# Shorter GpSimd subtractions, a short convolution kept in PSUM and an rsqrt with one instruction fewer, in a two-block transformer kernel

## The chip, the cores and the metric

The kernel runs on one core of one Trainium2 chip. The metric is the device time of one execution in microseconds; lower is better. Six parts of the core matter here: TensorE (PE; its weight loads are listed as PEld), VectorE (DVE), ScalarE (ACT), GpSimd (POOL), SyncE (SP), which issues most of the DMAs, and the two on-chip memories, SBUF and PSUM. GpSimd is used on SBUF tiles alone.

## The reference, cut to what matters

Input x has 512 tokens of 1024 features. Two layers of a first block and one layer of a second block follow one another, all in float32. Of the first block's mixer, the lines around the change are these:

```python
x_m, z, glu_a, glu_b = jnp.split(h @ w_in, ...)
x_c = jax.nn.silu(causal_depthwise_conv(x_m, w_conv_m, b_conv_m))   # 4 taps
q, k = einsum(x_c, w_q), einsum(x_c, w_k)
v = einsum(x_m, w_v)
h_m = sigmoid(z) * group_layer_norm(mlstm(q, k, v, gates))
a = glu_a * sigmoid(glu_b)
a = silu(group_layer_norm(causal_depthwise_conv(a, w_dw, b_dw)))    # 31 taps
y = concat([h_m, a]) @ w_out
```

A feed-forward stage (1024 to 4096 to 1024, squared ReLU) closes each layer. The second block has index attention over selected keys, window attention and a feed-forward stage. RMS and layer norms stand between the stages; each needs 1/sqrt of a mean.

## The kernel before, in words

**Products of split operands.** Each product is computed as three matmuls (mm3, lines 195 to 204). Both operands are split into a rounded part and a remainder. The rounded part is a ScalarE copy; the remainder is a subtraction on VectorE or GpSimd. For weights this is done in prep (173 to 180): a unit of 128 x 1024 arrives by DMA, ScalarE rounds it (177) and line 179 subtracts, on GpSimd for the units that the tables TUNE name under pool and on VectorE for the rest. AHEAD = 4 units are prepared ahead of use. For activations it is split (206 to 213); with pool set, line 210 runs on GpSimd. split_pair (695) sets it for the mixer's head inputs, 128 x 512 each, scores and split_hm set it where the table says so, and start sets it for every second feature tile.

**Stages.** mixer computes, feature-major, 8 tiles of x_m with their short convolution (ev_xm, 881), then heads, gates and the gated long convolution. The long convolution's taps (conv_gen, line 830) accumulate on VectorE into a PSUM bank of the ring py and are background work; conv_out norms each tile of it: transposes, rsqrt, ScalarE's scale (858), transposes back (862). values norms each head with rsqrt and ScalarE (802). In ev_xm, line 886 copies the product to xm on ScalarE, line 889 writes tap 0 with its bias into an SBUF tile, VectorE adds three taps, ScalarE takes Tanh (892). In the first layer, where mv[1] is 1, ScalarE adds 1 (894) and GpSimd multiplies (895); in the second layer one VectorE instruction does both.

**rsqrt** (215 to 236) is a chain of tiny VectorE instructions on up to four columns: halve, two integer instructions for a first guess, then two refining steps.

**What sets the order.** Paced (54) counts a rough time for each VectorE instruction, mm3 counts TensorE's. pump (132) issues background work (long-convolution taps, modulation sums at line 287, selection) while VectorE's count is no later than TensorE's plus slack. A scheduler then orders the instructions of each engine by priority (later, soon). Each engine works through its queue in order. Most weights are fetched from SyncE's queue, some modulation rows (298) from GpSimd's. PSUM has a ring p of five banks, py of two and pc of one; a product takes its bank when its first matmul is issued and gives it back after the last reader.

The lines shown as L68 in the profile are all VectorE instructions issued through Paced.

Of the kernel before, what the change touches and what calls it, by code (L numbers as in the profile page):

```python
# [21 lines left out]
MID = 3  # L22
CALM = True
# [17 lines left out]
NEG = -1e30  # L41
# [3 lines left out]
# the guess is 1.5 ** 0.2 / sqrt, for the cubic step to have a leading coefficient of 1  # L45
# [8 lines left out]
class Paced:  # L54
    """an engine whose instructions are counted, by their rough time"""
# [16 lines left out]
class Kern:  # L72
# [59 lines left out]
    def pump(self):  # L132
        """issue what fits in before VectorE would be later than TensorE"""
        again = True
        while again:
            again = False
            for b in (self.bg[-1:] + self.bg[:-1] if self.tune["af"] else self.bg):
                cost, at, cond = b[1]
                if self.pt < at or (cond and not cond()) or (cost and self.dt + cost > self.pt + self.tune["slack"]):
                    continue  # L140
                self.dt = max(self.dt, self.pt - 3) + cost
                self.step(b)
                again = True
                break

    def drain(self, done):
        """issue background work until done()"""
        while not done():
            for b in self.bg:
                cost, at, cond = b[1]  # L150
                if cond is None or cond():
                    self.dt += cost
                    self.step(b)
                    break
            else:
                raise RuntimeError("nothing left to drain")

# [1 line left out]
    def add_chunk(self, src, widths, pool=""):  # L159
        """pool: which of the remainders GpSimd computes"""  # L160
        o = 0
        for i, w in enumerate(widths):
            self.plan.append((src[:, o:o + w], w, str(i) in pool))
            o += w
# [8 lines left out]
    def prep(self, i):  # L173
        raw, w = self.units[i], self.plan[i][1]
        u = self.units[i] = self.tile("w", (128, 2, 1024), F32R)
        with self.later("prep"):
            self.nc.scalar.activation(u[:, 0, :w], raw[:, :w], AF.Copy)  # L177
            eng = self.nc.gpsimd if self.plan[i][2] else self.V
            eng.tensor_tensor(u[:, 1, :w], raw[:, :w], f32(u[:, 0, :w]), op=OP.subtract)  # L179
        self.prepped += 1  # L180
# [25 lines left out]
    def split(self, hi, lo, src, scale=None, pool=False):  # L206
        nc = self.nc
        if scale is None:
            nc.scalar.activation(hi, src, AF.Copy)  # L209
            (nc.gpsimd if pool else self.V).tensor_tensor(lo, src, f32(hi), op=OP.subtract)  # L210
        else:
            nc.scalar.activation(hi, src, AF.Copy if isinstance(scale, float) else AF.Identity, scale=scale)
            self.V.scalar_tensor_tensor(lo, src, scale, f32(hi), op0=OP.mult, op1=OP.subtract)

    def rsqrt(self, src, w, mul, add, tag=None):
        """1 / sqrt(src * mul + add), src [128, w]: a guess from the bits, a cubic and a quadratic step"""
# [12 lines left out]
        V.tensor_scalar(z.bitcast(I32), vh.bitcast(I32), 1, None, op0=OP.logical_shift_right)  # L229
        V.tensor_scalar(z.bitcast(I32), z.bitcast(I32), -1, RSQRT_GUESS, op0=OP.mult, op1=OP.add)  # L230
# [53 lines left out]
    def ada_sum(self, w, l, i):  # L284
        """mod[:, i] = w . silu(c), w the i-th 128 rows of w_ada^T"""
# [32 lines left out]
    def scale_cols(self, l, which):  # L318
        """g_pre * (1 + sc), and sh"""
# [7 lines left out]
    def gate_row(self, l, which):  # L327
        """gt * g_post, as a row on every partition"""
# [17 lines left out]
    def start(self, evacs):  # L346
        """the first normed operand by feature tile, as its scale and shift arrive, and the first products with it"""
# [91 lines left out]
    def norm_T(self, ii, xs, ss, G, sh, to):  # L439
        """rows of the token tiles from ii on, normed; transposed, scaled and split into hT two by two, as pend is worked off"""  # L440
# [48 lines left out]
    def feat(self, evacs, halves=False, hook=None, tag="p"):  # L489
        """128 outputs each: [128, T] = w^T h^T, handed to its evac"""  # L490
# [58 lines left out]
    def post_norm(self, l, which, nxt):  # L549
        """x += gt * rms_norm(y) * g_post; then the next normed operand"""  # L550
# [40 lines left out]
    def gate_weights(self, l):  # L591
        """Wq Wgq + Wk Wgk and Wv Wgv by head, as [feature, 8 gates]; in 4 steps"""
# [46 lines left out]
    def gates(self, l):  # L639
        """gate pre-activations by token -> log forget sums, and what the weights need; in 4 steps"""  # L640
# [89 lines left out]
    def weights_exp(self, h):  # L730
        """exp(a_s - M_t) for s <= t, by key tile"""
# [41 lines left out]
    def values(self, S, vt, h):  # L773
        """weighted sums of values, normed by head: [128 tokens, 4 tiles, 256]"""
# [42 lines left out]
    def conv_gen(self, l, inp, out):  # L817
        """the taps of the depthwise convolution, by channel tile"""
# [15 lines left out]
    def conv_out(self, l, c, yp, outs):  # L834
        """silu(norm over the 128 channels of the group)"""
# [35 lines left out]
    def mixer(self, l, nxt, halves=True):  # L871
# [9 lines left out]
        def ev_xm(j):  # L881
            def ev(p):
# [4 lines left out]
                y, th = self.t2(), self.t2()  # L887
# [5 lines left out]
                if self.tune["mv"][1]:  # L893
                    nc.scalar.activation(th, th, AF.Copy, bias=1.0)
                    nc.gpsimd.tensor_tensor(xc, th, y, op=OP.mult)
                else:
                    V.scalar_tensor_tensor(xc, th, 1.0, y, op0=OP.add, op1=OP.mult)
# [162 lines left out]
    def tok_proj(self, n, kks, evac):  # L1060
        """[128 tokens, n] = h w for each token tile"""
# [27 lines left out]
    def rotate(self, src, i, n, pool=False):  # L1089
        """rotary embedding of n heads of token tile i; src and result [128, n, 64]"""  # L1090
# [14 lines left out]
    def q_hold(self, i, p, hold, tag):  # L1105
        """query heads of a token tile, rotated: [tokens, head, rounded part and remainder]"""
# [6 lines left out]
    def q_turn(self, i, hold, qt, hps):  # L1113
        """token tiles i and i + 1 of two pairs of heads into qt"""
# [18 lines left out]
    def q_proj(self, tag):  # L1133
        """8 query heads: 4 tiles [rounded part; remainder of a head, 2 heads, T], once the turns are worked off"""
# [5 lines left out]
    def k_proj(self):  # L1140
        """index key, 2 + 2 key heads: [part twice; T] for the rounded part and the remainder"""
# [61 lines left out]
    def qk_mm(self, out, q, h, tk, k, keys):  # L1203
        """q . k from [q_h; q_l] and [k_h; k_h], [k_l; k_l]"""
# [24 lines left out]
    def select(self):  # L1229
        """in place of the scores: 0 for each query's 128 largest (the earliest among equals), NEG elsewhere"""  # L1230
# [12 lines left out]
    def scores_a(self, h, qt, kt):  # L1243
        """one head's probabilities over the selected keys, by query tile"""
# [51 lines left out]
    def scores_b(self, hp, qt, kt):  # L1296
        """two heads' probabilities in the window, by query tile"""
# [46 lines left out]
    def gate(self, t, tag):  # L1344
        """the next 128 gates, as tanh of their half"""
        self.feat([lambda p: self.nc.scalar.activation(t, p, AF.Tanh, scale=0.5)], tag=tag)

    def branch(self, j, w, o, tag="p"):
        """128 outputs of a branch: [128, T] = w^T o"""
# [178 lines left out]
# order of the 128-wide column tiles of w_in: 0-7 x_m, 8-15 z, 16-23 glu_a, 24-31 glu_b  # L1528
# [125 lines left out]
```

## Time and profile before

| what | value |
|---|---|
| median of 3 runs (range) | 2425.57 us (2423.27 to 2426.83) |
| profiled execution, first to last instruction | 2424.3 us, 1.3 us below the median |
| TensorE busy | 2252.7 us, 93% |
| VectorE busy | 1610.0 us, 66% |
| ScalarE busy | 976.7 us, 40% |
| GpSimd busy | 625.4 us, 26% |
| chain that ended last | PE 62%, DVE 24%, ACT 4%, POOL 1% |

The profiled execution lists no time of its own beside its span. Busy times are unions of the instructions' records on an engine. Matmuls are pipelined, so a busy TensorE isn't one at its peak. A wait is put down to the instruction whose semaphore came last.

### The profile page before, as it was taken

The numbers are of one execution on the slowest core, as the hardware profiler recorded it, in microseconds if no ns is written. First come the engines' busy times: TensorE is split into PE (matmuls) and PEld (weight loads), VectorE is DVE, ScalarE is ACT, GpSimd is POOL, SyncE is SP. The second block draws the span as 40 slices with busy tenths as digits, with TensorE's granted clock in tenths as the row PEclk, the third lists the DMA queues.
The fourth block names the chain that finished last, engine by engine and source line by source line (L and its number), as shares of the span: only waits on it lengthen the run. The fifth ranks groups of instructions, "written<-read, shape, count | busy, mean of one in ns | idle before, by whom it ended". The sixth has DMA issues, their size and how long they took to land.

```text
span 2424.3 us, 28416 instructions
## 1 busy us (share of the span) xinstructions
PE 2252.7 (93%) x10552; PEld 1828.9 (75%) x10552; DVE 1610.0 (66%) x2971; ACT 976.7 (40%) x1705; POOL 625.4 (26%) x408
## 2 busy tenths in 40 slices
PE   5988998899999998898897999999989999999998
PEld 4667776688888776776676888887877888888886
DVE  6899999755777669999956233347887435443444
ACT  3434554443232343455445333234436543422332
POOL 2733452313234243444322011012031231000000
PEclk9999999999999999999998999999999999999999
DMA  7523223526666422222133332223111223322222
GB/s 271 174 75 106 71 81 118 181 97 214 214 206 205 144 97 81 66 66 66 63 108 104 122 104 96 96 87 109 62 70 44 63 103 138 110 95 94 95 96 87
DMA packets 77754, 271.34 MB, mean 112 GB/s; under 512 B 9008, under 2 KB 9776, under 8 KB 77616
## 3 DMA queue, kind: packets, MB, share of 16 engines
q1 hardware_dynamic: 69840, 241.21, 29.9%
q0 software_dynamic: 7776, 28.32, 3.6%
q8 instruction: 83, 1.36, 0.2%
q14 instruction: 55, 0.45, 0.1%
HBM read 256.91 MB, written 12.58 MB: 111 GB/s over the span
## 4 chain that ended last, share of the span: by engine, by line
PE 62%; DVE 24%; ACT 4%; issue 2%; POOL 1%; DMA 1%; ACTq 0%; DVEq 0%; SPq 0%; POOLq 0%
PE p L197 19%; PE p L199 19%; PE p L198 19%; DVE p L830 7%; DVE c L68 5%; DVE cc L68 2%; DVE t L68 2%; DVE s L68 1%; DVE E L68 1%; PE p L466 1%; DVE w L68 1%; DVE e L68 1%; DVE ad L287 1%; DVE d L68 1%; DVE hT L68 0%
## 5 line engine op out<-in xcount | busy, mean ns | idle before, releaser
L179 POOL TENSOR_TENSOR w<-wr,w 128x1024 fp32r<-128x1024 f32 (+1 forms) x166 | 399.7, 2411 | 842.8 <-ACT w L177 739.3
L177 ACT ACTIVATE w<-wr 128x1024 fp32r<-128x1024 f32 (+1 forms) x353 | 368.9, 1047 | 572.1 <-PE p L199 517.2
L197 PE MATMUL p<-hT,w 128*128 128x512 f32 (+1 forms) x1504 | 582.7, 389 | 14.0 <-ACT hT L209 7.6
L198 PE MATMUL p<-hT,w 128*128 128x512 f32 (+1 forms) x1504 | 576.0, 383 | 8.0 <-DVE hT L68 5.6
L199 PE MATMUL p<-hT,w 128*128 128x512 f32 (+1 forms) x1504 | 578.1, 385 | 1.3 <-POOL w L179 1.3
L197 PE MATMUL p<-w,s 128*128 128x512 f32 (+1 forms) x1152 | 450.9, 392 | 2.4 <-ACT s L209 2.2
L198 PE MATMUL p<-w,s 128*128 128x512 f32 (+1 forms) x1152 | 449.4, 390 | 2.0 <-DVE w L68 2.0
L199 PE MATMUL p<-w,s 128*128 128x512 f32 (+1 forms) x1152 | 447.3, 390 | 1.1 <-DVE s L68 0.8
L68 DVE TENSOR_TENSOR w<-wr,w 128x1024 fp32r<-128x1024 f32 (+1 forms) x187 | 232.9, 1245 | 288.2 <-ACT w L177 288.1
L197 PEld LDWEIGHTS p<-hT,w 128*128 128x128 f32 x1504 | 289.5, 193 | 74.5 <-ACT hT L209 9.6
L830 DVE SCALAR_TENSOR_TENSOR p<-ga,ad,p 128x495 f32<-128x495 f32 (+25 forms) x480 | 339.2, 728 | 3.3 <-ACT p L825 2.3
L198 PEld LDWEIGHTS p<-hT,w 128*128 128x128 f32 x1504 | 289.3, 192 | 64.9 <-DVE hT L68 7.5
L199 PEld LDWEIGHTS p<-hT,w 128*128 128x128 f32 x1504 | 289.3, 192 | 59.4 <-POOL w L179 3.3
L197 PEld LDWEIGHTS p<-w,s 128*128 128x128 f32 x1152 | 217.6, 189 | 52.3 <-ACT s L209 2.9
L199 PEld LDWEIGHTS p<-w,s 128*128 128x128 f32 x1152 | 217.4, 189 | 51.0 <-DVE s L68 1.2
L198 PEld LDWEIGHTS p<-w,s 128*128 128x128 f32 x1152 | 217.4, 189 | 49.6 <-DVE w L68 2.5
L68 DVE TENSOR_TENSOR E<-p,E 128x512 f32<-128x512 f32 (+4 forms) x152 | 95.3, 639 | 138.2 <-PE p L199 111.8
L68 DVE SCALAR_TENSOR_TENSOR t<-p,t 128x512 f32<-128x512 f32 x96 | 66.0, 687 | 129.6 <-ACT t L1028 129.6
L287 DVE SCALAR_TENSOR_TENSOR ad<-ad,ad 128x1024 f32<-128x1024 f32 x80 | 115.5, 1450 | 39.2 <-DMA ad<-in_ada_dram 39.1
L1028 ACT ACTIVATE t<-p 128x512 f32<-128x512 f32 x96 | 56.7, 591 | 179.7 <-PE p L199 179.7
L68 DVE TENSOR_TENSOR s<-t,s 128x512 fp32r<-128x512 f32 (+1 forms) x100 | 110.9, 1109 | 9.5 <-ACT s L1030 4.7
L573 POOL TENSOR_TENSOR E<-E,s 128x512 f32<-128x512 f32 x32 | 46.0, 1445 | 175.2 <-ACT j L571 175.2
(273 smaller groups left out, 2805.2 us busy)
## 6 DMA issues: line engine op xcount, KB each, us to landing
wr<-in_ff_dram SPq DMA_DIRECT2D x128, 512.0 KB, 3.7
wr<-in_win_dram SPq DMA_DIRECT2D x64, 512.0 KB, 3.6
ad<-in_ada_dram POOLq DMA_DIRECT2D x54, 512.0 KB, 4.8
wr<-in_wout_dram SPq DMA_DIRECT2D x40, 512.0 KB, 3.6
wr<-in_up_dram SPq DMA_DIRECT2D x32, 512.0 KB, 3.6
wr<-in_down_dram SPq DMA_DIRECT2D x32, 512.0 KB, 3.7
ad<-in_ada_dram SPq DMA_DIRECT2D x26, 512.0 KB, 4.2
xd<-E SPq DMA_DIRECT2D x20, 512.0 KB, 2.7
```

The costliest lines, as they stand in the source:

```text
L68: return f(out, *a, **kw)
L177: self.nc.scalar.activation(u[:, 0, :w], raw[:, :w], AF.Copy)
L179: eng.tensor_tensor(u[:, 1, :w], raw[:, :w], f32(u[:, 0, :w]), op=OP.subtract)
L197: mm(out, lh, rh, start=first, stop=False)
L198: mm(out, lh, rl, start=False, stop=False)
L199: self.mm = mm(out, ll, rh, start=False, stop=last)
L287: return self.nc.vector.scalar_tensor_tensor(w, w, 1.0, self.cact, op0=OP.mult, op1=OP.mult, accum_out=m)
L466: nc.tensor.transpose(p[:, k, 128 * t:128 * t + 128], x[t][:, j * 128:(j + 1) * 128], self.ident)
L573: nc.gpsimd.tensor_tensor(y[:, h], y[:, h], row[:, h], op=OP.mult)
L830: V.scalar_tensor_tensor(y[:, d:], a[:, :T - d], w[:, o - d:o - d + 1], y[:, d:], op0=OP.mult, op1=OP.add)
L1028: nc.scalar.activation(r, p, AF.Relu)
```

## The change

Three edits. A constant PIECE = 256 is added. In prep and in split, a subtraction that GpSimd computes is issued in pieces of 256 columns (in split only where the source has two dimensions and more than 256 columns). In ev_xm the short convolution accumulates in the PSUM bank of its own product instead of an SBUF tile, and the last multiply is one VectorE instruction in both layers. In rsqrt, the shift and the multiply-add on integers become one multiply-add with the factor -0.5. The diff also strips comments, which moves line numbers.

```diff
+PIECE = 256
...
 def prep(self, i):
             self.nc.scalar.activation(u[:, 0, :w], raw[:, :w], AF.Copy)
-            eng = self.nc.gpsimd if self.plan[i][2] else self.V
-            eng.tensor_tensor(u[:, 1, :w], raw[:, :w], f32(u[:, 0, :w]), op=OP.subtract)
+            if self.plan[i][2]:
+                for o in range(0, w, PIECE):
+                    e = min(o + PIECE, w)
+                    self.nc.gpsimd.tensor_tensor(u[:, 1, o:e], raw[:, o:e], f32(u[:, 0, o:e]), op=OP.subtract)
+            else:
+                self.V.tensor_tensor(u[:, 1, :w], raw[:, :w], f32(u[:, 0, :w]), op=OP.subtract)
...
 def split(self, hi, lo, src, scale=None, pool=False):
             nc.scalar.activation(hi, src, AF.Copy)
-            (nc.gpsimd if pool else self.V).tensor_tensor(lo, src, f32(hi), op=OP.subtract)
+            if pool and len(src.shape) == 2 and src.shape[1] > PIECE:
+                for o in range(0, src.shape[1], PIECE):
+                    e = min(o + PIECE, src.shape[1])
+                    nc.gpsimd.tensor_tensor(lo[:, o:e], src[:, o:e], f32(hi[:, o:e]), op=OP.subtract)
+            else:
+                (nc.gpsimd if pool else self.V).tensor_tensor(lo, src, f32(hi), op=OP.subtract)
...
 def rsqrt(self, src, w, mul, add, tag=None):
-        V.tensor_scalar(z.bitcast(I32), vh.bitcast(I32), 1, None, op0=OP.logical_shift_right)
-        V.tensor_scalar(z.bitcast(I32), z.bitcast(I32), -1, RSQRT_GUESS, op0=OP.mult, op1=OP.add)
+        V.tensor_scalar(z.bitcast(I32), vh.bitcast(I32), -0.5, RSQRT_GUESS, op0=OP.mult, op1=OP.add)
...
 def ev_xm(j):
-                y, th = self.t2(), self.t2()
+                y, th = p, self.t2()
                 w = lambda d: self.cols[l][:, o + j * KM + KM - 1 - d:o + j * KM + KM - d]
                 nc.scalar.activation(y, p, AF.Identity, scale=w(0), bias=self.col(l, "b_conv_m", j))
                 for d in range(1, KM):
                     V.scalar_tensor_tensor(y[:, d:], xm[:, :T - d], w(d), y[:, d:], op0=OP.mult, op1=OP.add)
                 nc.scalar.activation(th, y, AF.Tanh)
-                if self.tune["mv"][1]:
-                    nc.scalar.activation(th, th, AF.Copy, bias=1.0)
-                    nc.gpsimd.tensor_tensor(xc, th, y, op=OP.mult)
-                else:
-                    V.scalar_tensor_tensor(xc, th, 1.0, y, op0=OP.add, op1=OP.mult)
+                V.scalar_tensor_tensor(xc, th, 1.0, y, op0=OP.add, op1=OP.mult)
```

## Rows read from the trace of the kernel before

**Rows 1.** Stretch, length, busy (count) of PE, PEld, DVE, ACT, POOL, clock, DMA share, GB/s
```profile
60.00:130.00 70.00, 63.28 (x277) 42.26 (x275) 61.03 (x68) 33.68 (x51) 48.32 (x25) 0.98 0.48 158
130.00:430.00 300.00, 268.46 (x1272) 216.47 (x1271) 283.57 (x607) 142.64 (x273) 110.61 (x76) 0.94 0.30 94
...
500.00:830.00 330.00, 330.00 (x1466) 270.08 (x1465) 213.92 (x239) 104.75 (x142) 106.49 (x86) 1.00 0.59 190
...
920.00:1230.00 310.00, 275.57 (x1327) 220.37 (x1326) 287.33 (x587) 142.84 (x272) 124.20 (x90) 0.96 0.20 66
```

**Rows 2.** Waits of TensorE, 130 to 430: us in total, times, longest
```profile
PE p L862 <- ACT tc L858: 6.8, 5, 2.6
...
PE p L810 <- ACT E L802: 5.7, 1, 5.7
```

**Rows 3.** The same view, 920 to 1230
```profile
PE p L862 <- ACT tc L858: 15.1, 7, 3.2
```

**Rows 4.** Timeline from 460 us: start, duration, engine, line, operation, tiles, count
```profile
464.76 4.64 POOL L179 TENSOR_TENSOR w<-wr,w 128x1024 fp32r<-128x1024 f32 x2
464.85 2.27 DVE L68 SCALAR_TENSOR_TENSOR c<-c 128x2 f32<-128x2 f32 x1
...
467.15 2.27 DVE L68 SCALAR_TENSOR_TENSOR c<-c,c 128x2 f32<-128x2 f32 x1
```

**Rows 5.** Tiles c and cc: duration ns minimum/median/maximum, first and last start, forms
```profile
L68 DVE TENSOR_SCALAR c<-c x132: 144/167/2351, 10.3 to 2417.8; 128x2 f32<-128x2 f32 x30, 128x2 int32<-128x2 int32 x28, 128x1 int32<-128x1 int32 x24, 128x4 int32<-128x4 int32 x20
...
L68 DVE TENSOR_SCALAR cc<-cc x48: 149/160/2373, 145.5 to 1237.2; 128x4 int32<-128x4 int32 x32, 128x4 f32<-128x4 f32 x16
```

**Rows 6.** Groups by shape, VectorE, 130 to 430: busy us, mean ns | idle before
```profile
L68 DVE TENSOR_TENSOR c<-c,c 128x4 f32<-128x4 f32 x20 | 8.8, 438 | 0.0
L68 DVE SCALAR_TENSOR_TENSOR cc<-cc,cc 128x4 f32<-128x4 f32 x21 | 8.7, 413 | 0.0
...
L68 DVE SCALAR_TENSOR_TENSOR d<-d,d 128x16 f32<-128x16 f32 x9 | 7.0, 772 | 0.0
...
L68 DVE TENSOR_SCALAR c<-c 128x4 int32<-128x4 int32 x8 | 5.6, 706 | 0.0
```

**Rows 7.** The same view, 920 to 1230
```profile
L68 DVE SCALAR_TENSOR_TENSOR cc<-cc,cc 128x4 f32<-128x4 f32 x21 | 13.4, 638 | 0.0
...
L68 DVE TENSOR_TENSOR c<-c,c 128x4 f32<-128x4 f32 x20 | 8.5, 424 | 0.0
...
L68 DVE SCALAR_TENSOR_TENSOR c<-c,c 128x4 f32<-128x4 f32 x12 | 7.2, 604 | 0.0
...
L68 DVE TENSOR_TENSOR cc<-cc 128x4 f32<-128x4 f32 x14 | 7.1, 508 | 0.0
```

**Rows 8.** Groups by shape, GpSimd, the whole span
```profile
L179 POOL TENSOR_TENSOR w<-wr,w 128x1024 fp32r<-128x1024 f32 x158 | 389.2, 2467 | 820.9 <-ACT w L177 717.5 <-DVE c L68 48.3 <-issue 27.7
...
L210 POOL TENSOR_TENSOR s<-e,s 128x512 fp32r<-128x512 f32 x4 | 5.2, 1300 | 4.1 <-ACT s L209 4.1
...
L210 POOL TENSOR_TENSOR s<-e,s 128x256 fp32r<-128x256 f32 x4 | 3.0, 758 | 0.6 <-ACT s L209 0.6
```

**Rows 9.** Groups by shape, VectorE, the whole span
```profile
L68 DVE SCALAR_TENSOR_TENSOR t<-p,t 128x512 f32<-128x512 f32 x96 | 66.0, 687 | 129.6 <-ACT t L1028 129.6
...
L68 DVE SCALAR_TENSOR_TENSOR t<-E,ad,t 128x511 f32<-128x511 f32 x16 | 20.3, 1268 | 11.1 <-ACT t L889 11.1
...
L830 DVE SCALAR_TENSOR_TENSOR p<-ga,ad,p 128x511 f32<-128x511 f32 x16 | 11.9, 743 | 2.3 <-ACT p L825 2.3
```

**Rows 10.** Groups by shape, GpSimd, 130 to 430 and 920 to 1230
```profile
L179 POOL TENSOR_TENSOR w<-wr,w 128x1024 fp32r<-128x1024 f32 x29 | 70.2, 2423 | 118.9 <-ACT w L177 94.3 <-issue 16.2 <-DMA wr<-in_win_dram 4.1
...
L179 POOL TENSOR_TENSOR w<-wr,w 128x1024 fp32r<-128x1024 f32 x36 | 87.1, 2421 | 163.0 <-ACT w L177 151.3 <-PE p L197 7.1 <-PE p L785 4.6
```

**Rows 11.** Timeline from 98 us
```profile
98.41 0.60 ACT L886 ACTIVATE E<-p 128x512 f32<-128x512 f32 x1 [5.16 <-PE p L199]
...
106.26 0.73 DVE L68 SCALAR_TENSOR_TENSOR t<-E,ad,t 128x509 f32<-128x509 f32 x1
```

## The prediction

> **What bounds the kernel now.** I read first the busy time by stretch, because the kernel has stages with different limits [rows 1]. In the feed-forward stretch from 500 to 830 us TensorE is busy for all of it, while VectorE has 116 us to spare: nothing that VectorE or GpSimd gains there can shorten it. In the two mixer stretches (130 to 430 and 920 to 1230 us, called A and B below) it is the other way round. VectorE is busy for 283.57 of 300 and 287.33 of 310 us, and TensorE stands still for 31.5 and 34.4 us. So VectorE sets the pace in A and B, and the 65.9 us in which TensorE idles there are the most that faster VectorE work can give back in them.
>
> Next, who TensorE waits for in A and B [rows 2, 3]. The largest groups are transposes that wait for ScalarE's line 858 (6.8 and 15.1 us) and line 802 (5.7 us in A). Both lines apply a norm whose scale comes from rsqrt, a chain of tiny VectorE instructions: the wait belongs to VectorE.
>
> Then a stretch at a stage's border, where rsqrt runs with GpSimd beside it [rows 4]. Two of GpSimd's 1024-column subtractions follow each other from 464.76 to 469.40 us. A two-column VectorE instruction that starts at 464.85 lasts 2.27 us, the next one, at 467.15, again 2.27: the first ends in the middle of the pair, the second 0.02 us behind its end. Undisturbed such an instruction takes 0.16 to 0.17 us (medians in [rows 5]); the longest in those rows are 2.35 and 2.37 us. So VectorE waits for a whole GpSimd instruction, and between two of GpSimd's that stand back to back it gets in once.
>
> How much is that in A and B? I take the four largest groups of tiny instructions of each and subtract 0.16 us from each mean. In A [rows 6]: 20 x 0.28 + 21 x 0.25 + 9 x 0.61 + 8 x 0.55 = 20.7 us. In B [rows 7]: 21 x 0.48 + 20 x 0.26 + 12 x 0.44 + 14 x 0.35 = 25.5 us. Together 46 us of VectorE's time in A and B is waiting for GpSimd, by these eight rows alone. The smaller groups of the same kind add to it; I leave them out of the sum and set them against what the halving below may miss.
>
> **Part 1, pieces of 256 columns.** A subtraction of 1024 columns lasts 2.47 us and becomes four of 0.76; one of 512 lasts 1.30 and becomes two [rows 8]. The longest wait falls from about 2.4 to 0.76 us, a factor of 0.31. Against that GpSimd is occupied for 4 x 0.76 = 3.03 us instead of 2.47, so VectorE meets it 1.23 times as often: together 0.38, a saving of 62%, 28 us. That is the upper end for these groups. It holds where other VectorE work stands between two links of a chain, the long convolution's taps above all, which work in PSUM and run beside the pieces. Where tiny instructions follow one another directly, each can meet another piece, as at 465 us [rows 4]; there four pieces cost as much as one long instruction and a little more. The lower end is therefore a loss in proportion to the longer occupation: 46 x 0.23 = 11 us. I take a half, a saving of 23 us, because A and B are full of taps.
>
> GpSimd's own extra time is 0.56 us a unit. It has idled 820.9 us in front of this line, most of it for ScalarE's rounding [rows 8], and units are prepared four ahead, so I cost it at nothing. If that cover were gone, the matmuls that take the remainder would wait. At the borders between stages I cost the pieces at nothing too: chains there are bare, so gain and loss cancel; bounds from [rows 4] are a gain of 4 us (the two long waits) and a loss of 1 us a border.
>
> [...] GpSimd's rows go the same way: 2 x 0.758 - 1.300 = 0.22 us a cut [rows 8]. [...]
>
> **Part 2, the short convolution in PSUM.** There are 16 tiles with three taps each. A tap of this kind takes 1.268 us on average from SBUF to SBUF; a tap of the same length that accumulates in PSUM takes 0.743 [rows 9]. 48 x 0.525 = 25 us of VectorE time goes, nearly all of it waiting. But where? Most lies in 60 to 130 us and in the halves stage before 920. In 60 to 130 VectorE is busy 61.0 and TensorE 63.3 of 70 us [rows 1], so at most 6.7 us can come back. The first mixer also gains eight multiplies on VectorE (0.687 us each by the nearest row of that shape with a PSUM source [rows 9], 5.5 us), and loses an add on ScalarE and a multiply on GpSimd for each. I take 4 us for that stretch, and 2 us for the taps that reach into B. ScalarE's first step writes PSUM instead of SBUF; no row shows PSUM to PSUM, and a tenth of a microsecond either way on 16 instructions is within the range.
>
> **Part 3, rsqrt.** The integer rows count 28 + 24 + 20 + 32 = 104 instructions, two a call, so 52 calls [rows 5]. One of 0.16 us goes from each: 8.3 us. Those in A and B shorten the engine that is the bound, those at the borders and at the end a bare chain. The few beside other waits win nothing: I take 7 us.
>
> **What the reordering may do.** The order of background work is counted out from rough VectorE costs (Paced, pump). One instruction fewer in rsqrt and one more in ev_xm shift that count, and taps land elsewhere. Nothing in the trace prices this; the nearest row is a tap of 0.743 us [rows 9], and some ten places moved make 7 us either way.
>
> **The sum.** 23 + 4 + 2 + 7 = 36 us. I add 6 for the smaller groups of waits in A and B, which are certain to exist and halve like the others: 42. From the profiled span of 2424.3 us that leaves 2382.3. The median of the runs is 1.3 us above the span, so I predict 2383.6, rounded 2384 us. The 29 us of parts 1 and the smaller groups fit inside TensorE's 65.9 us of idling.
>
> **Rivals.**
> First, the pieces win little: VectorE and GpSimd take turns, each link of a chain meets a piece, or TensorE's fixed order does not hand the gain on. For it: [rows 4] show the turns. Against it: in A and B taps stand between the links. Then parts 2 and 3 stay (13 us) and a sixth of the other 29: about 2408.
> Second, the fixed time of the pieces comes on the path, since the remainder of each unit is ready later. A and B hold 29 and 36 units [rows 10]; three cuts each at 0.22 us make 43 us on GpSimd. It decides once GpSimd's queue has no idle time left in front of a unit. Then 42 gained and 43 lost give 2427, no change. Against it stand the 118.9 and 163.0 us of idling in front of these units [rows 10]. [...]
> Third, slower: the bank. A short-convolution tile now keeps its product's PSUM bank until the last multiply. One product's copy starts at 98.41 us and its last tap at 106.26 [rows 11], so with Tanh and the multiply the hold is about 10 us and not two. In the stretch where nothing holds TensorE up a matmul takes 330 / 1466 = 0.225 us [rows 1], so a product's 24 take 5.4 us; with the five banks of this ring the other four products leave some 21 us before TensorE has to wait for a bank; from that hold on it decides. If it did at each of the 16 tiles, TensorE would wait for three taps, a Tanh and a multiply, 3 x 0.743 + 0.6 + 0.687 = 3.5 us each: 56 us lost against 42 gained, 2440. It speaks against it that the taps themselves get shorter.
>
> [...]
>
> **How the numbers follow.** A measurement of this kernel can tell 0.2%, about 5 us. The forecast has 0.55, the small gain 0.23, the fixed time on the path 0.10, the bank 0.12. The first two are faster by over 0.2%: 0.78; the third is no change: 0.10; the fourth is slower: 0.12. The range starts where TensorE's idling in A and B is all gone and parts 2 and 3 outside them add some 9 us: 2425.6 - 65.9 - 9 = 2351, rounded 2350. Its upper end takes in the small gain and half of the third case: 2425.
>
> **What would show it.** GpSimd's subtractions appear as 256 columns at about 0.76 us, four times as many. The means in [rows 6, 7] fall to about 0.3 us and no tiny instruction lasts longer than about 1 us beside line 179's work. The short taps stand at 0.74 us. TensorE's idling in A and B falls from 66 to about 35 us. The forecast is wrong if those means stay, if TensorE idles for GpSimd's remainders, or if matmuls of the short-convolution stages wait for a bank.

## The result and the profile after

| | before | after |
|---|---|---|
| median of the runs, us | 2425.06 (2423.27 to 2426.83, 4 runs) | 2338.33 (2335.55 to 2339.5, 4 runs) |
| span of the profiled execution, us | 2424.3 | 2336.8 |

The ratio is 0.9636, with a 95% interval from 0.9622 to 0.9649: 88 us less by the ratio (87 by the medians), where 42 had been forecast. The time is below the range too. The sign was right and so was the mechanism of part 1; the size was not. Two executions far slower than the rest, one of e8's four (3899.51 us) and one of e12's four (7702.12 us), are left out of the ratios below but not of the medians, which would be 2333.64 and 2356.32 us without them.

The page of the changed kernel, its busy time by engine and its chain:

```profile
PE 2224.5 (95%) x10552; PEld 1811.9 (78%) x10552; DVE 1484.2 (64%) x2927; ACT 972.6 (42%) x1697; POOL 709.3 (30%) x934
...
PE 75%; DVE 14%; ACT 4%; issue 2%; POOL 2%; DMA 1%; SPq 0%; ACTq 0%; DVEq 0%; POOLq 0%
```

TensorE has now 95% of the span, and the chain that ended last runs through it for 75%. GpSimd has become busier, by what the cuts cost it: 709.3 us for 625.4.

Busy time by stretch, to set beside [rows 1]. Stages lie earlier now, so A and B are cut out by what happens in them, from the last Tanh of each layer's short convolution to the last tap of its long one: 127 to 393 and 907 to 1137 us here.

```profile
core 0: us, PE busy (x) PEld busy (x) DVE busy (x) ACT busy (x) POOL busy (x), PEclk, DMA share, GB/s
60.00:130.00 70.00, 69.49 (x307) 47.16 (x308) 51.46 (x80) 31.83 (x48) 40.29 (x56) 1.00 0.49 158
127.00:393.00 266.00, 251.93 (x1243) 206.35 (x1242) 246.76 (x586) 139.98 (x270) 130.10 (x184) 0.98 0.35 108
907.00:1137.00 230.00, 225.77 (x1140) 184.71 (x1139) 219.59 (x529) 120.29 (x239) 125.18 (x192) 1.00 0.24 74
```

The same cut of the kernel before:

```profile
134.00:423.00 289.00, 257.46 (x1220) 207.77 (x1220) 273.19 (x584) 138.66 (x268) 110.15 (x75) 0.94 0.28 91
955.00:1220.00 265.00, 238.16 (x1157) 193.62 (x1156) 250.99 (x538) 122.83 (x241) 110.17 (x83) 0.97 0.19 63
```

A is 266 us long and was 289, B 230 and was 265. TensorE stands still for 14.1 and 4.2 us in them, where it stood still for 31.5 and 26.8. And its granted clock rose, from 0.94 and 0.97 to 0.98 and 1.00: its own work in the two got shorter, 477.7 us for 495.6, though its matmuls there are not fewer (2383 for 2377). The stretch from 60 to 130 us, where TensorE was busy for 63.28, has 69.49.

The groups of GpSimd that were cut, by shape ([rows 8]):

```profile
L182 POOL TENSOR_TENSOR w<-wr,w 128x256 fp32r<-128x256 f32 x648 | 493.5, 794 | 722.1 <-ACT w L178 629.4 <-DVE c L69 48.2 <-issue 38.4
L218 POOL TENSOR_TENSOR s<-E,s 128x256 fp32r<-128x256 f32 x80 | 60.1, 784 | 4.7 <-ACT s L214 4.6
```

A piece takes 0.79 us, where 0.76 had been read off. The first tap of the short convolution, for [rows 9]:

```profile
L69 DVE SCALAR_TENSOR_TENSOR p<-E,ad,p 128x511 f32<-128x511 f32 x16 | 12.0, 749 | 10.2 <-ACT p L898 10.2
```

It takes 749 ns, where it took 1268 and 743 had been forecast. A group of tiny instructions in A, for [rows 6]:

```profile
L69 DVE TENSOR_TENSOR c<-c,c 128x4 f32<-128x4 f32 x20 | 5.4, 269 | 0.0
```

And two in B, for [rows 7]:

```profile
L69 DVE SCALAR_TENSOR_TENSOR cc<-cc,cc 128x4 f32<-128x4 f32 x21 | 5.8, 275 | 0.0
...
L69 DVE TENSOR_TENSOR c<-c,c 128x4 f32<-128x4 f32 x20 | 5.0, 251 | 0.0
```

They come from 438, 638 and 424 ns. The tile cc of [rows 5], with the minimum, median and maximum of its durations:

```profile
L69 DVE TENSOR_SCALAR cc<-cc x32: 148/159/743, 177.6 to 1156.3; 128x4 f32<-128x4 f32 x16, 128x4 int32<-128x4 int32 x16
```

The longest lasts 743 ns, one piece, where it was 2373. On c thirteen still take more than 0.9 us, each beside a GpSimd instruction of 512 columns that was not cut: twelve beside post_norm's multiplication (line 582), one beside line 1115.

The waits of TensorE in A, for [rows 2]:

```profile
PE p L202 <- DVE e L69: 6.1, 4, 2.3
PE p L819 <- DVE cc L69: 4.9, 1, 4.9
...
PE p L871 <- ACT tc L867: 0.7, 1, 0.7
```

And in B, for [rows 3]:

```profile
PE p L871 <- ACT tc L867: 1.6, 4, 1.0
```

Line 871 is line 862 of before. Its transposes behind the norm of the long convolution waited for 6.8 and 15.1 us; they wait for 0.7 and 1.6. What is left in A is above all four waits for VectorE's tile e (line 202) and one wait of 4.9 us for a tiny instruction on cc (line 819, line 810 of before).

### The profile page after: what moved, and what is told of

Same layout as the page of the kernel before. It is cut to its first block, busy times and chain, and to the rows that moved or that the text cites. A ratio compares the mean times of both kernels' runs of the same rounds, so it can differ in the third digit from the quotient of the medians.

```text
span 2336.8 us, 28930 instructions
## 1 busy us (share of the span) xinstructions
PE 2224.5 (95%) x10552; PEld 1811.9 (78%) x10552; DVE 1484.2 (64%) x2927; ACT 972.6 (42%) x1697; POOL 709.3 (30%) x934
## 3 DMA queue, kind: packets, MB, share of 16 engines
q8 instruction: 83, 1.36, 0.2%
## 4 chain that ended last, share of the span: by engine, by line
PE 75%; DVE 14%; ACT 4%; issue 2%; POOL 2%; DMA 1%; SPq 0%; ACTq 0%; DVEq 0%; POOLq 0%
PE p L202 23%; PE p L204 23%; PE p L203 23%; DVE p L839 3%; DVE c L69 3%; DVE E L69 1%; POOL w L182 1%; PE p L475 1%; DMA ad<-in_ada_dram 1%; DVE w L69 1%; DVE s L69 1%; ACT w L178 1%; PE p L621 1%; PE p L1211 1%; DVE hT L69 1%
## 5 line engine op out<-in xcount | busy, mean ns | idle before, releaser
L182 POOL TENSOR_TENSOR w<-wr,w 128x256 fp32r<-128x256 f32 x648 | 493.5, 794 | 722.1 <-ACT w L178 629.4
L202 PEld LDWEIGHTS p<-hT,w 128*128 128x128 f32 x1504 | 286.2, 191 | 74.7 <-ACT hT L214 9.6
L839 DVE SCALAR_TENSOR_TENSOR p<-ga,ad,p 128x495 f32<-128x495 f32 (+24 forms) x480 | 339.3, 728 | 6.6 <-ACT p L834 5.5
L203 PEld LDWEIGHTS p<-hT,w 128*128 128x128 f32 x1504 | 286.3, 190 | 67.3 <-POOL hT L218 6.5
L204 PEld LDWEIGHTS p<-hT,w 128*128 128x128 f32 x1504 | 286.1, 190 | 57.8 <-POOL w L182 3.8
L69 DVE SCALAR_TENSOR_TENSOR t<-p,t 128x512 f32<-128x512 f32 x96 | 65.9, 687 | 127.8 <-ACT t L1033 127.8
L296 DVE SCALAR_TENSOR_TENSOR ad<-ad,ad 128x1024 f32<-128x1024 f32 x80 | 107.2, 1345 | 53.6 <-DMA ad<-in_ada_dram 53.6
L69 DVE TENSOR_TENSOR s<-t,s 128x512 fp32r<-128x512 f32 (+1 forms) x100 | 102.1, 1021 | 12.8 <-ACT s L1035 7.3
```

The lines of the kernel that those rows point to most:

```text
L69: return f(out, *a, **kw)
L182: self.nc.gpsimd.tensor_tensor(u[:, 1, o:e], raw[:, o:e], f32(u[:, 0, o:e]), op=OP.subtract)
L202: mm(out, lh, rh, start=first, stop=False)
L203: mm(out, lh, rl, start=False, stop=False)
L204: self.mm = mm(out, ll, rh, start=False, stop=last)
L296: return self.nc.vector.scalar_tensor_tensor(w, w, 1.0, self.cact, op0=OP.mult, op1=OP.mult, accum_out=m)
```

## The experiments

Each is timed against the kernel before, with the runs of before on the same chip. "Before" and "changed" name the two kernels; "saved" is one minus the ratio, times the median of before.

### The parts alone

**e1_pieces**: before, with part 1 of the change only.

```diff
-            eng = self.nc.gpsimd if self.plan[i][2] else self.V
-            eng.tensor_tensor(u[:, 1, :w], raw[:, :w], f32(u[:, 0, :w]), op=OP.subtract)
+            if self.plan[i][2]:
+                for o in range(0, w, PIECE):
...
```

> The kernel before with GpSimd's subtractions in pieces of 256 columns alone; VectorE's order of instructions is that of before, instruction for instruction. Theory W (the change wins because VectorE waits less for GpSimd): 45 to 60 us faster, since VectorE's records beside GpSimd shrink in both mixers. Rival R (much of the change's gain is the new order of background work that the other two parts bring): at most 25 us faster.

Measured: 2357.22 us, ratio 0.9704 [0.9682, 0.9726], 72 us saved [67, 77]. It is more than either theory wanted, on the side of the waits. (The profiled execution, the slowest of the four, is 66.5 us shorter than that of before.) This run settles the main question, because it leaves VectorE's order as it was: in the two traces all 2971 of them stand in the same sequence, by operation, tiles and shape, and only their times differ. Here are A (140 to 400) and B (928 to 1161), to be set beside the cut of before above:

```profile
140.00:400.00 260.00, 250.06 (x1229) 202.75 (x1228) 241.83 (x584) 138.35 (x268) 130.93 (x185) 0.99 0.33 103
928.00:1161.00 233.00, 228.99 (x1156) 187.72 (x1156) 221.40 (x537) 122.59 (x241) 129.60 (x195) 1.00 0.23 71
```

With 584 and 537 instructions (before: 584 and 538) VectorE is busy for 241.83 and 221.40 us instead of 273.19 and 250.99: 31.4 and 29.6 less, 61.0 together. A and B are shorter by 29 and 32 us, also 61. So what VectorE no longer waits is what the stages lose, one to one. The instructions on the tile cc alone, A and B, in the kernel before:

```profile
134.00:423.00 289.00, 38.42 (x133) 10.52 (x28) 0.94 0.28 91
955.00:1220.00 265.00, 46.90 (x131) 9.04 (x24) 0.97 0.19 63
```

And in this run:

```profile
140.00:400.00 260.00, 27.69 (x133) 10.53 (x28) 0.99 0.33 103
928.00:1161.00 233.00, 29.70 (x131) 9.04 (x24) 1.00 0.23 71
```

With the same view for the tiles c and d that makes, in us of VectorE:

| tile, instructions in A and B | A before | A, e1 | B before | B, e1 |
|---|---|---|---|---|
| cc, 133 and 131 | 38.42 | 27.69 | 46.90 | 29.70 |
| c, 97 and 97 | 32.34 | 23.06 | 31.10 | 20.96 |
| d, 18 and 18 | 10.46 | 3.92 | 5.10 | 4.42 |
| sum | 81.22 | 54.67 | 83.10 | 55.08 |

54.6 us of the 61.0 come from these three tiles of tiny instructions.

For TensorE the 61 us have two halves that differ in kind. Its idling falls from 31.5 + 26.8 = 58.3 to 9.9 + 4.0 = 13.9 us: 44.4. Its busy time falls from 495.6 to 479.1 us, though it executes eight matmuls more (2385 for 2377): 16.6 us, while the granted clock goes from 0.94 and 0.97 to 0.99 and 1.00. Before, of the four stretches in [rows 1], the clock was lowest in the two in which TensorE stood still most; with less standing still it came back.

**e2_psum**: before, with the short convolution's part only.

```diff
-                y, th = self.t2(), self.t2()
+                y, th = p, self.t2()
...
-                if self.tune["mv"][1]:
-                    nc.scalar.activation(th, th, AF.Copy, bias=1.0)
-                    nc.gpsimd.tensor_tensor(xc, th, y, op=OP.mult)
-                else:
-                    V.scalar_tensor_tensor(xc, th, 1.0, y, op0=OP.add, op1=OP.mult)
+                V.scalar_tensor_tensor(xc, th, 1.0, y, op0=OP.add, op1=OP.mult)
```

> The kernel before with the short convolution in its product's PSUM bank alone (with the last multiply on VectorE in both layers). W: 15 to 25 us faster, the waits of 48 taps. R: 30 us or more, most of it in the long mixer stretches where no short tap runs. If the bank were a cost: slower than before.

Measured: 2414.48 us, ratio 0.9941 [0.992, 0.9962], 14 us saved [9, 19]; just under what was expected, with the interval reaching into it. (The profiled execution, the slowest of the four, is 6.9 us shorter than that of before.) From 60 to 130 us TensorE is busy for 68.88 us instead of 63.28. By the last Tanh of the first short convolution the kernel is 8.5 us ahead (125.2 us for 133.7). In the long convolution of A it gives 8 of them back; presumably the new order of background work places taps elsewhere, which no run separates. In the second short convolution it gains 10 again. No wait of TensorE for a product's bank shows from 40 to 130 us.

What TensorE no longer waits for in the first short convolution is not VectorE's taps. These are TensorE's two longest waits from 40 to 130 us in the kernel before; e2 has neither:

```profile
PE p L612 <- DMA ga<-in_wqT_dram: 3.9, 1, 3.9
PE p L633 <- POOL E L895: 2.0, 1, 2.0
```

The second is for the multiply that GpSimd did. The first is for a load that stands late in SyncE's queue, behind the fetch of a weight unit that waits for GpSimd. GpSimd's timeline in the kernel before, and SyncE's:

```profile
73.00 2.41 POOL L179 TENSOR_TENSOR w<-wr,w 128x1024 fp32r<-128x1024 f32 x1
```

```profile
75.44 0.33 SPq L170 DMA_DIRECT2D wr<-in_win_dram  x1
75.82 0.90 SPq L604 DMA_DIRECT2D ga<-in_wqT_dram  x2
```

The fetch (line 170) goes out 0.03 us behind the end of the subtraction, and the load of ga follows it. In e2 the load stands one weight fetch earlier in the queue and goes out at 67.38 us; the fetch that it passed goes out at 74.45. The edit doesn't touch SyncE's instructions: the scheduler's order came out another way with it. The changed kernel has the early order as well, e1 and e12 have the late one.

In the second layer VectorE did the multiply before as well. There one wait for VectorE's last tile is gone, of the kernel before:

```profile
PE p L633 <- DVE E L68: 7.0, 1, 7.0
```

So this part acts in three ways: shorter taps, the multiply on VectorE, and an order of SyncE's queue that fell out of it. The waits speak for the last two in the first layer and for the taps in the second; no run times one of them alone.

**e3_rsqrt_order**: before, with both integer instructions of rsqrt executed, but the first issued past the counting of VectorE's time, so that the count that places background work is the one of the shorter rsqrt.

```diff
-        V.tensor_scalar(z.bitcast(I32), vh.bitcast(I32), 1, None, op0=OP.logical_shift_right)
+        self.nc.vector.tensor_scalar(z.bitcast(I32), vh.bitcast(I32), 1, None, op0=OP.logical_shift_right)
```

> The kernel before with both integer instructions of the rsqrt guess executed, but one of them left out of the count that places background work; so VectorE's order is that of the kernel with the shorter rsqrt, and no instruction is saved. W: within 5 us of before. R: 15 us or more faster.

Measured: 2433.26 us, ratio 1.0016 [1.0005, 1.0028], 4 us lost [1, 7]. The reordering in this run costs a little and brings nothing. It is not quite the reordering of the shorter rsqrt: of VectorE's 2867 instructions outside the integer ones, e3 has another one than before in 437 places of the sequence, and another one than e12, which has the shorter rsqrt, in 744.

**e4_no_pieces**: changed, so that no remainder is cut: parts 2 and 3 without part 1.

```diff
-PIECE = 256
+PIECE = 4096
```

> The changed kernel with GpSimd's subtractions whole again (PSUM and rsqrt parts kept). W: 25 to 35 us faster than before, so that the pieces are worth 50 to 60 us of the 87. R: 50 us or more faster than before.

Measured: 2404.71 us, ratio 0.9903 [0.9878, 0.9927], 24 us saved [18, 30], 1 us under what was expected. With e2's 14 the rsqrt is worth some 10; with the changed kernel's 88 the pieces are worth some 64 on top of the other two, close to their 72 alone.

**e12_no_psum**: changed, with e2's diff taken back, so without the short convolution's part.

```diff
-                y, th = p, self.t2()
+                y, th = self.t2(), self.t2()
...
```

> The changed kernel without the short convolution's part (pieces and the shorter rsqrt guess only). Theory A (the short convolution's part is worth in the changed kernel what it was worth alone, 14 us, since its taps got shorter by reading PSUM): 2338 + 14, so 2348 to 2356. Theory O (alone and here it acts mainly through the order that it moves and through the wait behind GpSimd that the pieces shorten anyway): 2334 to 2346.

Measured: 2357.06 us, ratio 0.9702 [0.9666, 0.9738], 72 us saved [64, 81]. Against the 88 of the changed kernel the short convolution's part is worth about 16, the size that theory A has, though the interval is wide. Its reason, the shorter taps, is not shown by the size. The two profiled executions differ by 10.8 us at the end of the first short convolution alone, and there e12 has the waits of before again, 6.8 us for ga and 3.3 us for GpSimd's multiply, and the changed kernel neither. Against e1, which has the pieces alone, the shorter rsqrt shows no gain here. Its 10 us of e4 are therefore not sure: some of them may have been waits that the pieces shorten as well.

### The size of a piece, and which pieces count

**e5_piece512**, **e6_piece128** and **e11_piece384**: changed, with PIECE at 512, 128 and 384. **e7_prep_only**: changed, with the cutting in split switched off, so that only the weights' remainders come in pieces.

```diff
-PIECE = 256
+PIECE = 512
```

```diff
-            if pool and len(src.shape) == 2 and src.shape[1] > PIECE:
+            if pool and len(src.shape) == 2 and src.shape[1] > 4096:
```

> The changed kernel with pieces of 512 columns in place of 256 (the activations' subtractions of 512 stay whole). Theory W (VectorE waits at most for one of GpSimd's instructions, so the gain goes with their length): the longest wait is 1.30 us, between 2.4 and 0.76; 55 to 70 us faster than before, against 25 with whole units and 87 with 256. Rival P (the gain comes from the hand-over of a unit in parts, whatever their length): 80 us or more.

> The changed kernel with pieces of 128 columns. A piece of 128 takes 0.47 us, so a unit takes 8 x 0.47 = 3.8 us of GpSimd instead of 3.0. W: waits shrink a little more, 83 to 97 us faster than before. Rival F (the fixed time of more pieces comes on the path, or VectorE meets a piece at every link): 70 us or less.

> Pieces of 384 columns (1024 in 384, 384, 256; 512 in 384, 128). Theory W (what VectorE waits is the rest of one piece, and each piece costs GpSimd a fixed 0.2 us): between 256 (2338) and 512 (2380), near the middle, 2348 to 2370. Theory E (the gain comes from two pieces fitting between two VectorE chains, that is from 256 or less): no better than 512, 2375 or more. If the fixed cost already weighs at 256: 2338 or less.

> The changed kernel with pieces of 256 for weights alone; the activations' subtractions of 512 and 384 columns on GpSimd stay whole (1.30 us). W: 75 to 85 us faster than before, since these are a fifth of GpSimd's time in the mixers and half as long as a whole unit. P: 85 us or more (nothing lost).

| PIECE | time, us | ratio and interval | saved, us |
|---|---|---|---|
| 512 | 2379.76 | 0.9807 [0.9784, 0.9829] | 47 |
| 384 | 2348.32 | 0.9678 [0.9662, 0.9695] | 78 |
| 256 (changed) | 2338.33 | 0.9636 [0.9622, 0.9649] | 88 |
| 128 | 2367.81 | 0.9755 [0.9733, 0.9777] | 59 |
| 256 for weights alone (e7) | 2345.46 | 0.9662 [0.964, 0.9685] | 82 |

GpSimd's weight subtractions in the run with 512 columns:

```profile
L182 POOL TENSOR_TENSOR w<-wr,w 128x512 fp32r<-128x512 f32 x324 | 434.6, 1364 | 800.0 <-ACT w L178 689.6 <-DVE c L69 48.2 <-issue 43.7
```

And in the one with 128:

```profile
L182 POOL TENSOR_TENSOR w<-wr,w 128x128 fp32r<-128x128 f32 x1296 | 613.9, 511 | 648.7 <-ACT w L178 578.0 <-DVE c L69 47.8 <-issue 21.0
```

e5 saved less than both theories asked for: the hand-over of a unit in parts, which wanted 80 us, fell, and the 55 to 70 us of theory W were too much. On c, cc and d VectorE is busy for 135.2 us in A and B (461 instructions; 128 to 409 and 931 to 1182 us), in the changed kernel for 100.8 (474). e11 lies at the lower edge of its range. e7 agrees with its expectation: nearly all of the gain comes from the weights.

e6 was meant to tell whether still shorter waits help or whether the fixed time of a piece takes over. In time it went where the fixed cost should have sent it: four pieces of 511 ns cost GpSimd 2.04 us for the 1.36 of one of 512 columns. But TensorE nowhere in A or B waits for a remainder of GpSimd's that its view lists. (From 10 to 140 us, ahead of A, it does: 8.3 us for line 218 and 2.9 for line 182, 11.2 together, where the changed kernel has 5.4 and 1.5; e6's last Tanh there comes 6.2 us later.) The largest of its waits in A (133 to 418 us):

```profile
PE p L819 <- ACT E L811: 8.9, 1, 8.9
```

And what ScalarE's line 811 waits for in turn:

```profile
ACT E L811 <- DVE c L69: 9.3, 2, 8.9
```

The 8.9 us go back to one VectorE instruction. GpSimd's timeline around it:

```profile
347.14 3.81 POOL L218 TENSOR_TENSOR s<-E,s 128x128 fp32r<-128x128 f32 x9
350.90 6.75 POOL L182 TENSOR_TENSOR w<-wr,w 128x128 fp32r<-128x128 f32 x16
```

And VectorE's:

```profile
347.53 10.14 DVE L69 TENSOR_TENSOR c<-c,ga 128x4 f32<-128x4 f32 x1
357.60 0.73 DVE L839 SCALAR_TENSOR_TENSOR p<-ga,ad,p 128x501 f32<-128x501 f32 x1
```

An instruction on four columns lasted 10.14 us. It came while the first of 25 pieces was running and did not get in between any two of them: it ended 0.02 us behind the last, at 357.65. In B one of 512 columns took 6.66 us in the same way (975.99 to 982.65). A is 285 us long with 128 columns and 266 in the changed kernel; TensorE's wait for that one instruction is 8.9 of the 19 us, and another 7 are its own busy time (258.8 us for 251.9, at a granted clock of 0.95 for 0.98). The rest of e6's loss I have not taken apart.

In the changed kernel the usual picture is this one, at the border from 1197 us:

```profile
1197.16 3.46 POOL L182 TENSOR_TENSOR w<-wr,w 128x256 fp32r<-128x256 f32 x5
1197.27 0.65 DVE L69 SCALAR_TENSOR_TENSOR c<-c,c 128x2 f32<-128x2 f32 x1
1197.95 0.65 DVE L69 TENSOR_TENSOR c<-c 128x2 f32<-128x2 f32 x1
1198.63 0.65 DVE L69 TENSOR_TENSOR c<-c,c 128x2 f32<-128x2 f32 x1
1199.31 0.65 DVE L69 SCALAR_TENSOR_TENSOR c<-c,c 128x2 f32<-128x2 f32 x1
```

Five pieces, and one link of the chain between each two: 0.65 us a link, where [rows 4] show 2.27. So the two engines take turns as a rule. Of the 2927 VectorE instructions of the changed kernel 15 last over 1.5 us longer than the shortest of their form, 14 of them in the first feed-forward stage (the next experiment) and one in B, a multiplication of 512 columns that took 2.36 us from 958.32. What made the instruction at 347.53 lose its turn is open.

### A lost turn behind an issue

**e9_loads_from_sync**: in the first feed-forward stage VectorE's subtractions s<-t,s take 1.9 us on average in the changed kernel. The group, 500 to 790 us:

```profile
L69 DVE TENSOR_TENSOR s<-t,s 128x512 fp32r<-128x512 f32 x25 | 48.6, 1942 | 4.3 <-ACT s L1035 3.2
```

GpSimd's timeline around one of them:

```profile
563.45 0.57 POOL L307 DMA_DIRECT2D ad<-in_ada_dram  x1 [1.97 <-DVE ad L296]
564.04 2.83 POOL L182 TENSOR_TENSOR w<-wr,w 128x256 fp32r<-128x256 f32 x4
```

And VectorE's:

```profile
563.86 3.57 DVE L69 TENSOR_TENSOR s<-t,s 128x512 fp32r<-128x512 f32 x1
```

It starts while GpSimd issues a load (L307) and waits through all four pieces behind it. Ten of the 25 start during such an issue, and each takes 3.56 to 3.58 us. An eleventh, at 747.69, takes 3.18 us: it starts 0.2 us into the first piece behind an issue. The others take 0.67 to 0.82. The edit has SyncE issue these loads:

```diff
-        dict(slack=0.0, tap=400, prep=20, fetch=-50, ada=100, aq=0, ...
+        dict(slack=0.0, tap=400, prep=20, fetch=-50, ada=100, aq=1, ...
```

> The changed kernel, with the loads of the modulation weights in the first feed-forward stage (L307) issued by SyncE in place of GpSimd. In the changed kernel 25 VectorE subtractions s<-t,s of that stage (500 to 790 us) take a mean of 1942 ns, and the longest of them began in the last 0.17 us of such an issue on GpSimd and then waited through four pieces. Theory D (a VectorE instruction that arrives while GpSimd issues a load loses its turn to the whole run of pieces behind it): the mean falls to 1.1 us or less and none waits over 1.5 us. Rival T (the turn is lost through the moment of arrival, whatever stands on GpSimd): the mean stays at 1.5 us or more. Either way TensorE sets that stage, so the kernel is within 8 us of the changed one (2330 to 2346); an order of SyncE's queue that delays weights would show as more than that.

Measured: 2336.63 us, ratio 0.9626 [0.9612, 0.9641]; not to be told from the changed kernel. The group:

```profile
L69 DVE TENSOR_TENSOR s<-t,s 128x512 fp32r<-128x512 f32 x25 | 19.5, 781 | 17.1 <-ACT s L1035 16.7
```

From 1942 to 781 ns, with none over 1.14 us: theory D holds. 29 us of VectorE's time went, and the kernel's time did not move, because TensorE sets that stage: in the changed kernel it is busy for all of the 314 us from 467 to 781, as in [rows 1]. The same kind of waiting that set the pace in A and B was worth nothing in this stage.

### Further cuts

**e8_multiply_pieces**: changed, and post_norm's multiplication on GpSimd in pieces too. **e10_multiply_and_sync**: e8 and e9 together.

```diff
-                nc.gpsimd.tensor_tensor(y[:, h], y[:, h], row[:, h], op=OP.mult)
+                for o in (0, PIECE):
+                    q = slice(nh * 512 + o, nh * 512 + o + PIECE)
+                    nc.gpsimd.tensor_tensor(y[:, q], y[:, q], row[:, q], op=OP.mult)
```

> The changed kernel with the 32 multiplies of 512 columns on GpSimd at the stages' ends (post_norm) in pieces of 256 as well. The norm's chain of tiny VectorE instructions runs beside them. W: 87 to 92 us faster than before; if turn-taking eats it in these bare chains: 84 to 87.

> The run before this one together with post_norm's multiplication in pieces of 256 (e8_multiply_pieces, 2334.88). If the two are independent the sum holds: 2335 plus what e9_loads_from_sync gave against 2338, within 3 us. If the shorter multiplications only gained because they moved work about, nothing of the 4 us is left (2338 or more plus that).

Measured: e8 2334.88 us, ratio 0.9615 [0.9593, 0.9636], 93 us saved, 1 over what was expected; e10 2335.77 us, ratio 0.9621 [0.9607, 0.9635]. Both intervals overlap that of the changed kernel, so neither is shown to beat it. The sum that e10 was to give, 2333, is met within 3 us; but the other outcome, some 2336 or more with nothing left of e8's 4 us, lies closer, and the run does not tell the two apart. All three of the tried additions have medians between 2334 and 2337: none shows a further gain.

## Why the prediction was right in kind and wrong in size

- **What bounds the kernel: right.** VectorE set the pace in A and B by waiting for GpSimd. e1, with nothing reordered on VectorE, shows its waits and the stages' length fall by the same 61 us. The list of TensorE's waits that the prediction calls the largest passes over some of that size: in the same views of before, 6.3 us for the tile d (line 669) in A, and in B 7.5 us at line 810 and 7.0 at line 633. The first two go back to VectorE's tiny instructions too.
- **Part 1's term: here the prediction failed.** It put 23 us on the pieces and 6 on the smaller groups, 29 in A and B; e1 has 61 there. Two factors were low. The first is "I take a half". The eight groups' waiting over 0.16 us was 46.2 us and is in e1 20 x 0.069 + 21 x 0.046 + 9 x 0.055 + 8 x 0.098 = 3.6 in A and 20 x 0.183 + 20 x 0.075 + 12 x 0.104 + 14 x 0.107 = 7.9 in B: 11.5, so 75% of it is gone, beyond the upper end of 62%. The quarter that is left is less even than the 0.31 of the shorter wait; the extra 1.23 for meeting GpSimd more often did not show. The second, and larger, is the 6 us for the smaller groups. The eight rows gave 34.7 of the 61 us, where 23 had been put, and everything else gave about 26. The four rows of A are 58 instructions of the 248 that A has on c, cc and d; the sum should have been made over whole tiles, not over the four largest groups of a listing. An estimate of it: with 0.16 us for each, and 0.28 and 0.40 us for the statistics instructions among them, which take that long in these traces, the three tiles would be busy in A and B for some 93 us. They were for 164.3 before and are for 109.8 in e1: about 71 us of waiting, not 46, and some 77% of it gone.
- **The cap of 65.9 us: wrong in kind.** "The most that faster VectorE work can give back" left out that TensorE's own work took longer in the stretches in which it stood still much: 495.6 us for 2377 matmuls in A and B before, 479.1 for 2385 in e1. In [rows 1] the column of the clock had the sign of it, 0.94 and 0.96 against 1.00. Of e1's 61 us in A and B 44.4 came out of idling and 16.6 out of TensorE's busy time. The lower end of the range, 2350, was built on that cap.
- **Borders at nothing: right within some microseconds.** e1's profiled execution starts 5.9 us late into A, gains 4.7 between A and B and 7.1 behind B.
- **GpSimd's own extra time at nothing: wrong ahead of A.** e1 loses its 5.9 us there. Until 62 us TensorE waits 5.4 us for GpSimd's line 218, where before waited 2.3 (line 210). Then a weight fetch in SyncE's queue waits for GpSimd's longer work, the load of ga behind it goes out at 81.47 us, where before had 75.82, and TensorE waits for it:

```profile
PE p L622 <- DMA ga<-in_wqT_dram: 7.0, 1, 7.0
```

- **Part 2, 6 us: too low, and in the first mixer for another reason.** 14 alone, about 16 in the changed kernel. The taps are as short as forecast: 749 ns on average in PSUM, where e1, with the pieces but the taps from SBUF to SBUF, still has 938 to 1019. But in 60 to 130 us, priced at 4 by VectorE's time, e2 gains 8.5 where two waits end: 2.0 us for the multiply that GpSimd loses, which had been named and not priced, and 3.9 us for a load that moved up in SyncE's queue, which the prediction does not have and which is luck. The other step that failed is the 2 us for the second mixer: the halves stage before B was seen and not costed, and it gives about 10, 7.0 of them the one wait for VectorE at line 633.
- **Part 3, 7 us: about right without the pieces (10), not shown with them.**
- **Reordering, 7 us either way: about held.** e3 loses 4, A in e2 loses 8.
- **First rival (the pieces win little): fell.** Turns are taken, at 256 columns, one link a piece and 0.65 us a link. Where e6 lost most in A, a link lost its turn to a whole row of pieces and took 10.14 us.
- **Second rival (fixed time on the path): fell at 256 as a whole.** The price of 0.22 us a cut, from GpSimd's durations in [rows 8], held: 2 x 0.794 - 1.364 = 0.22 by the pieces of 256 and 512 columns. But TensorE waits only 1.5 us for line 182's remainders in the whole span; what GpSimd's time cost came ahead of A, as said of e1. At 128 the kernel is slower again: in A by the lost turn for 8.9 of 19 us, ahead of A in part by waits for GpSimd's remainders; the rest is open.
- **Third rival (the bank): fell.** These are all the waits of TensorE that the view lists from 40 to 130 us in the changed kernel; none is for a bank of a product:

```profile
PE p L203 <- POOL hT L218: 3.6, 2, 3.1
PE p L855 <- ACT tc L848: 0.5, 1, 0.5
```

- **The signs: most came.** The means of the groups fell to 0.25 to 0.28 us, and TensorE's idling in A and B to 18.3 us, half of the 35 forecast. One did not: beside line 182's work an instruction on eight columns (G, 128x8) took 4.01 us from 624.95 on, in the stage of e9 and behind an issue.

## What to carry to other kernels

Where a trace shows one engine waiting out whole instructions of another, as here (2.27 us a link beside 1024 columns, 0.65 beside pieces of 256), the length of the instruction of the engine with time to spare is a cost to the other: cut it, and look for the size by trial, since here too small a piece lost again (88 us saved with 256 columns, 59 with 128). Sum such waiting over whole tiles and stretches, at the undisturbed duration of each form, before pricing a change; the largest groups of a listing held 46 of some 71 us here. Follow the other engine's time along the queues too: ahead of A, TensorE's wait for a load (3.9 us before, 7.0 in e1) was in part a wait for GpSimd. And where TensorE is granted less than its full clock, don't take its idle time for the limit of what can come back: of e1's 61 us in A and B, where before had 0.94 and 0.97, 16.6 came out of its busy time.

## What had not been expected of the hardware

VectorE does not always get in between two GpSimd instructions that stand back to back. In one group of the changed kernel the ten instructions that came while GpSimd issued a DMA all waited through the subtractions behind it (3.57 us with four pieces; gone when SyncE issued the loads), and with pieces of 128 columns one of four columns waited 10.14 us through a row of pieces without any issue ahead of it. Why that one lost its turn, when others beside the same line did not, the runs do not settle.

TensorE's granted clock went with its idling here over whole stages: 0.94 in A with 31.5 us of standing still in 289, 0.99 in e1 with 9.9 us in 260. Within A of before the clock was not one and the same: it was 1.00 from 134 to 154 us; then TensorE stood still from 153.4 to 159.7, and from 159 to 164 it was granted 0.50. A matmul of 128 x 512 on line 197 took 0.39 us just ahead of that wait, 0.63 to 0.77 behind it, and 0.39 again from 166.44 us on.
